# A gated hybrid decoder layer on one core: chunk states ordered ahead of VectorE's next work, output products one head later, silu and small copies on ScalarE, later modulation in blocks of 512 columns

## The chip, the cores and the metric

The kernel runs on one core of a Trainium2 chip. The metric is the device time of an execution in microseconds, as the median of runs. The engines are TensorE (PE in the views; PEld is its weight load), VectorE (DVE), ScalarE (ACT), GpSimd (POOL) and SyncE (SP), whose queue issues most transfers. Each engine takes its instructions in order.

## The reference

One layer for a prompt of 512 tokens and 64 sample tokens (8 sequences of 8), width 1024, all in 32 bits:

```python
mod = jax.nn.silu(c) @ w_ada + b_ada                  # shift1 scale1 gate1 shift2 scale2 gate2
u = x * (1 + sc1) + sh1
z = u @ w_in                                          # pool | q | f | i | out_gate | gate_A | gate_B
q = silu(z_q); f = lb + (1 - lb) * sigmoid(z_f); k = 1 - f; v = z_i      # 8 heads of 128
# per head, in chunks of 64 tokens, b = cumsum(log f) in the chunk:
att = tril((q * exp(b)) @ (k * exp(-b)).T);  o_intra = att @ v
S_c = exp(b_last) * S_(c-1) + (k * exp(b_last - b)).T @ v                # chunk states
o = o_intra + (q * exp(b)) @ S_(c-1)
y = o * rsqrt(mean(o * o) + eps) * hgrn_norm_w * silu(z_og)
merged = sigmoid(z_ga) * (y_pool @ w_a) + sigmoid(z_gb) * (y @ w_b)
x = layer_norm(ALPHA * x + g1 * (merged @ w_out))
h = x * (1 + sc2) + sh2
x = layer_norm(ALPHA * x + g2 * ((silu(h @ w_gate) * (h @ w_up)) @ w_down))
```

## The kernel before

Every large product is made in parts: a 32-bit matrix is split into a rounded high part (ScalarE's cast, tiles whi, hq) and a low rest (VectorE or GpSimd, tiles wlo, lq), and three products of the parts are added. On top of it `fast` (L217 to L250) makes two 1024-wide products at once by seven products of half size, p1 to p7, instead of eight; each has 12 matmuls of 288 columns (line L217). Its sums run on VectorE (L230), the first copy on ScalarE (L232); the seven results go through four banks of PSUM, tiles f. The callers hand in work to be written between the products: `mid` after the third, `end` after the fifth. `fast_w` loads the weights of the next pair by SyncE (L178) and prepares their sums on GpSimd (tiles st, L197 to L205) and their splits on all three (L172, L173); three buffers whi and wlo are shared by all, so a split waits until PE has left the one before.

In the loop over heads, pass h makes f and q of head h with one such pair and v and g (the output gate) with a second, while the recurrence of head h - 1 stands between: `hg1` transposes (L615 to L635), `hg2` makes the products within chunks, then the eight chunk states S one after another on VectorE (L663, each from the one before) and the sample states sn, `hg3` the outputs with their square root (L685 to L700), `hg4` turns the outputs back and multiplies by the gate. For head h, `ev_f` takes the sigmoid of f, runs the decay product as a scan (L559), three reciprocals (L562), kd (L564), GpSimd's kl (L566, L567) and its split klx; `ev_q`, `ev_qd`, `ev_i` and `ev_og` do the same for q, v (split vx) and g. `stack3` makes the splits klx and vx of the 64 sample columns.

Eight gate pairs follow. The first two carry the last head, the other six carry the rest of the modulation (`ada`, L339): shift2, scale2, gate1 and gate2, in 16 blocks of 256 columns. The feed-forward part (`ffn`) comes after the first layer norm, then the last product and norm.

The order on each engine is not the order of the code: a scheduler sets it when the program is built, by its own estimate of times; dependencies come from tiles. `tc.high_priority` lets instructions go ahead where they are ready; `tc.issue_after(ins)` keeps what a block writes for the engine of `ins` behind it. Line numbers are those of the kernel before; the changed kernel's lie up to some 30 lower or higher.

Of the kernel before, what the change touches and what calls it, by code (L numbers as in the profile page):

```python
# [73 lines left out]
def trunk(tc, consts, x_prompt, x_sample, state_pool, state_hgrn, c_prompt, c_sample,  # L74
# [254 lines left out]
    gada = {G1: t_(dr, [P, 4, 256], "gada1"), G2: t_(dr, [P, 4, 256], "gada2")}  # L329

    def ada(blk, pl_, psp, tag, raw=None):
# [12 lines left out]
        if G1 <= m < SH2 or m >= G2:  # L344
            base = G1 if m < SH2 else G2
            sp.dma_start(out=gada[base][:, (m - base) // 2], in_=ev)
            return
# [290 lines left out]
    def hg2(h):  # L638
# [36 lines left out]
        sp.dma_start(out=nhgrn_s[0, :, h].rearrange("b k v -> k b v"), in_=sn)

    def hg3(h):
# [616 lines left out]
```

## Time and profile before

| what | value |
|---|---|
| median of 3 runs | 1057.97 us (1055.69 to 1061.18) |
| profiled execution | 1058.36 us |
| its span, first to last instruction | 1056.6 us |
| mean granted clock of TensorE | 0.974 |
| PE busy | 987.5 us, 93% |
| VectorE busy | 828.6 us, 78% |
| ScalarE busy | 484.1 us, 46% |
| GpSimd busy | 368.6 us, 35% |

The span is what the trace shows; the profiled execution is 1.8 us longer than it. The stages, in us from the span's start: modulation, first products and pooling to 102; head 0's end and the first pass to 125; six passes to 341; the last head and gates 0 and 1 to 398; gates 2 to 7 with the later modulation to 490; the products with w_a, w_b and w_out and the first norm to 654; feed-forward products to 894; the last product and norm to the end. A busy share over the whole span hides that these stages have different limits, so it has to be read for each.

### The profile page before, as it was taken

To read this page: it belongs to the slowest core of one execution; us is meant where nothing else is said; L and a number is where in the kernel's file an instruction comes from. 1 tells how busy PE (TensorE), PEld (TensorE's weight loads), DVE (VectorE), ACT (ScalarE), POOL (GpSimd) and SP (SyncE) were. 2 spreads that over 40 slices of the span, in tenths; PEclk is the share of its full clock that TensorE was granted. 3 is DMA by queue.
4 is the path that set the end of the run, shared out by engine and by line. 5 is a ranking of instruction groups with operands and counts; after the bars stand their busy time and mean duration, and the time that the engine had idled before them with its cause. 6 is when DMAs were issued, how large, how long until landed. Compare 5 with 4: busy or idle time off the path is not lost.

```text
span 1056.6 us, 17662 instructions
## 1 busy us (share of the span) xinstructions
PE 987.5 (93%) x6803; PEld 897.7 (85%) x6803; DVE 828.6 (78%) x1433; ACT 484.1 (46%) x867; POOL 368.6 (35%) x269
## 2 busy tenths in 40 slices
PE   5999888989899899999988998999999999999993
PEld 3689888989899897788987677999999999788882
DVE  3563899879989966446899598999999999957428
ACT  3454564665466563334334344544434435633322
POOL 0013666657757554555364011112212210000004
PEclk7999999989999999999999999999999999999997
DMA  8940223323233229882324800232332333432202
GB/s 272 294 141 28 80 86 101 99 65 102 81 103 97 69 83 289 255 274 91 110 66 144 239 21 20 62 99 83 99 100 81 100 101 104 135 120 81 80 20 90
DMA packets 167143, 120.58 MB, mean 114 GB/s; under 512 B 4253, under 2 KB 154809, under 8 KB 167051
## 3 DMA queue, kind: packets, MB, share of 16 engines
q1 hardware_dynamic: 164719, 113.98, 35.9%
q10 hardware_dynamic: 2340, 5.47, 1.7%
q8 instruction: 53, 0.87, 0.3%
q14 instruction: 31, 0.25, 0.1%
HBM read 111.15 MB, written 8.40 MB: 113 GB/s over the span
## 4 chain that ended last, share of the span: by engine, by line
PE 65%; DVE 19%; DMA 6%; issue 4%; ACT 3%; POOL 2%; SPq 0%; DVEq 0%; POOLq 0%; ACTq 0%
PE b L217 24%; PE f L217 13%; DVE wlo L173 4%; PE b L1139 4%; PE b L1138 4%; PE b L1137 4%; DMA ada<-in_w_ada 3%; PE zp L421 3%; PE z L154 3%; DMA raw<-in_w_in 1%; PE s L339 1%; PE b L1143 1%; DVE S L663 1%; PE b L1142 1%; DVE g L230 1%
## 5 line engine op out<-in xcount | busy, mean ns | idle before, releaser
L172 ACT CAST whi<-st 128x512 fp32r<-128x512 f32 x184 | 109.0, 617 | 102.1 <-POOL st L203 25.2
L173 DVE TENSOR_TENSOR wlo<-st,whi 128x512 fp32r<-128x512 f32 x140 | 126.8, 927 | 8.8 <-ACT whi L172 4.2
L217 PE MATMUL f<-uh,whi 128*128 128x288 f32 x352 | 107.3, 305 | 0.0
L217 PE MATMUL f<-ul,whi 128*128 128x288 f32 x352 | 106.2, 302 | 0.0
L217 PE MATMUL f<-uh,wlo 128*128 128x288 f32 x352 | 106.0, 301 | 0.0
L197 POOL TENSOR_TENSOR st<-raw 128x512 f32<-128x512 f32 x36 | 50.3, 1398 | 155.4 <-DVE wlo L173 58.6
L112 DVE TENSOR_TENSOR wlo<-raw,whi 128x1024 fp32r<-128x1024 f32 (+1 forms) x49 | 57.9, 1181 | 35.9 <-ACT whi L111 35.3
L172 ACT CAST whi<-raw 128x1024 fp32r<-128x1024 f32 x46 | 48.3, 1049 | 78.0 <-PE f L217 37.4
L198 POOL TENSOR_TENSOR st<-st,raw 128x512 f32<-128x512 f32 x46 | 62.2, 1353 | 51.0 <-issue 49.5
L111 ACT CAST whi<-raw 128x1024 fp32r<-128x1024 f32 (+1 forms) x49 | 47.9, 978 | 65.6 <-PE b L1139 20.0
L1139 PE MATMUL b<-whi,hl 128*128 128x512 f32 (+1 forms) x198 | 72.6, 367 | 0.0
L1138 PE MATMUL b<-whi,hl 128*128 128x512 f32 (+1 forms) x198 | 72.5, 366 | 0.0
L1137 PE MATMUL b<-wlo,hl 128*128 128x512 f32 (+1 forms) x198 | 72.3, 365 | 0.0
L217 PEld LDWEIGHTS f<-uh,whi 128*128 128x128 f32 x352 | 67.4, 191 | 3.5 <-issue 1.6
L217 PEld LDWEIGHTS f<-ul,whi 128*128 128x128 f32 x352 | 67.3, 191 | 2.7 <-issue 2.5
L217 PEld LDWEIGHTS f<-uh,wlo 128*128 128x128 f32 x352 | 67.1, 191 | 2.1 <-issue 1.6
L203 POOL TENSOR_TENSOR st<-raw,st 128x512 f32<-128x512 f32 x26 | 40.6, 1561 | 75.5 <-DVE wlo L173 74.2
L173 DVE TENSOR_TENSOR wlo<-raw,whi 128x1024 fp32r<-128x1024 f32 x46 | 62.7, 1363 | 2.4 <-ACT whi L172 2.3
L173 POOL TENSOR_TENSOR wlo<-st,whi 128x512 fp32r<-128x512 f32 x44 | 59.0, 1358 | 11.2 <-ACT whi L172 5.3
L1206 POOL TENSOR_TENSOR x<-x,lg 128x640 f32<-128x640 f32 (+2 forms) x4 | 5.9, 1468 | 160.0 <-ACT x L1197 160.0
L217 PE MATMUL b<-bh,whi 128*128 128x288 f32 x184 | 55.4, 301 | 2.1 <-ACT bh L172 2.1
L217 PE MATMUL b<-bh,wlo 128*128 128x288 f32 x184 | 54.8, 299 | 0.0
(464 smaller groups left out, 3304.4 us busy)
## 6 DMA issues: line engine op xcount, KB each, us to landing
raw<-in_w_in SPq DMA_DIRECT2D x52, 512.0 KB
ada<-in_w_ada SPq DMA_DIRECT2D x48, 512.0 KB
raw<-in_w_gate SPq DMA_DIRECT2D x22, 512.0 KB
raw<-in_w_down SPq DMA_DIRECT2D x22, 512.0 KB
raw<-in_w_up SPq DMA_DIRECT2D x12, 512.0 KB
rawu<-in_w_up SPq DMA_DIRECT2D x10, 512.0 KB
s<-in_state_hgrn SPq DMA_DIRECT2D x8, 512.0 KB
out<-sn SPq DMA_DIRECT2D x8, 512.0 KB
```

The lines of the kernel that those rows point to most:

```text
L111: act.copy(out=hi[:, :n], in_=raw[:, :n])
L112: eng.tensor_tensor(out=lo[:, :n], in0=raw[:, :n], in1=hi[:, :n].bitcast(F32), op=ALU.subtract)
L154: mm = pe.matmul(out=ps[:, GA0 + c0:GA0 + c1], lhsT=a[:, kt * P:(kt + 1) * P], rhs=x[:, kt, c0:c1], start=first and i == 0, stop=last and ...
L172: act.copy(out=hi, in_=src)
L173: return eng.tensor_tensor(out=lo, in0=src, in1=hi.bitcast(F32), op=ALU.subtract)
L197: pool.tensor_tensor(out=s1, in0=a21, in1=a22, op=ALU.add)
L198: pool.tensor_tensor(out=s2, in0=s1, in1=a11, op=ALU.subtract)
L203: eng.tensor_tensor(out=s4, in0=a12, in1=s2, op=ALU.subtract)
L217: pe.matmul(out=ps, lhsT=x[:, k * P:(k + 1) * P], rhs=y[:, k], start=first and k + i == 0, stop=last and k == 3 and i == 2)
L1137: pe.matmul(out=o, lhsT=xh, rhs=lo, start=first, stop=False)
L1138: pe.matmul(out=o, lhsT=xl, rhs=hi, start=False, stop=False)
L1139: return pe.matmul(out=o, lhsT=xh, rhs=hi, start=False, stop=last)
```

## The change

Four things are done. On ScalarE, silu takes the place of a sigmoid that VectorE multiplied by its argument, for q, the output gate and the feed-forward gate, and the plain copies of `stack3` (klx, vx) move from VectorE to ScalarE. In a head, the chunk states get priority, and VectorE's sample sums and its whole second pair of products (with `ev_q`) are ordered behind the last state; `hg3` moves from after the third product of that pair to after the fifth, `hg4` from the end of the pass to the next pass (in gate 0 for head 6); the square root and reciprocal are taken once for prompt and samples. The later modulation runs in eight blocks of 512 columns, two in each of gates 2 to 4, one in gates 5 and 6 and none in gate 7, with two buffers of 1 MB in place of three of 0.5 MB; the tiles of gate 7 are allotted after they are closed.

```diff
     def ada_load(pl_, blk):
-            raw = t_(pl_, [P, 4, 256], "ada", bufs=8 if pl_ is s0 else 3)
+            raw = t_(pl_, [P, 4, 256], "ada", bufs=8)
...
-    gada = {G1: t_(dr, [P, 4, 256], "gada1"), G2: t_(dr, [P, 4, 256], "gada2")}
+    gada = {G1: t_(dr, [P, D], "gada1"), G2: t_(dr, [P, D], "gada2")}
...
-    q0_ = act.activation(out=q0, in_=z[:, ZR], func=AF.Sigmoid)
-    dve.tensor_tensor(out=q0, in0=z[:, ZR], in1=q0, op=ALU.mult)
+    q0_ = act.activation(out=q0, in_=z[:, ZR], func=AF.Silu)
...
     def stack3(x, tag, his, lo):
         for i in his:
-            dve.tensor_copy(out=o[:, :, 32 * i:32 * i + 32], in_=xs_)
+            act.copy(out=o[:, :, 32 * i:32 * i + 32], in_=xs_)
...
     def ev_q(h, q):
-            x = t_(ep, [P, T], "tmp", bufs=4)
-            act.activation(out=x, in_=q, func=AF.Sigmoid)
-            dve.tensor_tensor(out=q, in0=q, in1=x, op=ALU.mult)
+            act.activation(out=q, in_=q, func=AF.Silu)
...
     def ev_og(h, g):
-        s = t_(ep, [P, T], "tmp", bufs=4)
-        act.activation(out=s, in_=g, func=AF.Sigmoid)
-        dve.tensor_tensor(out=g, in0=g, in1=s, op=ALU.mult)
+        act.activation(out=g, in_=g, func=AF.Silu)
...
     def hg2(h):
-        act.copy(out=S[:, 0], in_=ps[0][:, 0:P])
-        for c in range(1, NCH):
-            o = (c // 2) * P
-            dve.scalar_tensor_tensor(out=S[:, c], in0=S[:, c - 1], scalar=s["p"][:, c * CH + CH - 1:c * CH + CH],
-                                     in1=ps[c % 2][:, o:o + P], op0=ALU.mult, op1=ALU.add)
+        with tc.high_priority():
+            act.copy(out=S[:, 0], in_=ps[0][:, 0:P])
+            for c in range(1, NCH):
+                o = (c // 2) * P
+                end = dve.scalar_tensor_tensor(out=S[:, c], in0=S[:, c - 1], scalar=s["p"][:, c * CH + CH - 1:c * CH + CH],
+                                               in1=ps[c % 2][:, o:o + P], op0=ALU.mult, op1=ALU.add)
...
-            dve.tensor_tensor(out=sn[:, 4 * r:4 * r + 4], in0=ps.rearrange("p (b v) -> p b v", b=4),
-                              in1=sn[:, 4 * r:4 * r + 4], op=ALU.add)
+            with tc.issue_after(end.ins):
+                dve.tensor_tensor(out=sn[:, 4 * r:4 * r + 4], in0=ps.rearrange("p (b v) -> p b v", b=4),
+                                  in1=sn[:, 4 * r:4 * r + 4], op=ALU.add)
+        return end
...
     def hg3(h):
-            act.activation(out=ms[:n, a:b], in_=ms[:n, a:b], func=AF.Sqrt, scale=1.0 / P, bias=epsr[:n])
-            dve.reciprocal(out=ms[:n, a:b], in_=ms[:n, a:b])
+        act.activation(out=ms, in_=ms, func=AF.Sqrt, scale=1.0 / P, bias=epsr)
+        dve.reciprocal(out=ms, in_=ms)
+        for x, n, o, a, b in tiles:
             dve.tensor_tensor(out=o, in0=x[:n, :(b - a) * P].rearrange("p (i v) -> p i v", v=P), in1=bcast(ms[:n, a:b], P),
                               op=ALU.mult)
...
+    def ada_late(m, pl_):
+        ps = st_()
+        for st in range(2):
+            raw = t_(pl_, [P, 4, 512], "ada", bufs=2)
+            sp.dma_start(out=raw, in_=w_ada[0][st * 512:(st + 1) * 512, m * P:m * P + 512].rearrange("(k p) n -> p k n", p=P))
+            for g in range(4):
+                pe.matmul(out=ps[32 * g:32 * g + 32], lhsT=cpad[:, st * 4 + g, :], rhs=raw[:, g, :],
+                          start=st == 0, stop=st == 1, tile_position=(0, 32 * g))
+        ev = t_(pl_, [P, 512], "adaev")
+        dve.tensor_copy(out=ev, in_=ps)
...
     for h in range(1, NH):
         f, q = (t_(ep, [P, T], "tmp", bufs=4) for i in range(2))
-        fast_u(f, q, lambda: hg1(h - 1), lambda: ev_f(h, f))
-        hg2(h - 1)
-        ev_q(h, q)
-        v, g = vg()
-        fast_u(v, g, lambda: hg3(h - 1), lambda: (ev_qd(h), ev_i(h, v)))
-        hg4(h - 1)
+        def mid():
+            if h > 1:
+                hg4(h - 2)
+            hg1(h - 1)
+
+        fast_u(f, q, mid, lambda: ev_f(h, f))
+
+        with tc.issue_after(hg2(h - 1).ins):
+            ev_q(h, q)
+            v, g = vg()
+            fast_u(v, g, None, lambda: (hg3(h - 1), ev_qd(h), ev_i(h, v)))
         ev_og(h, g)
...
-    gate(0, lambda: hg1(NH - 1))
+    gate(0, lambda: (hg4(NH - 2), hg1(NH - 1)))
...
     for m in range(2, KT):
-        for i in range(3 if m < 6 else 2):
-            ada(ada_todo.pop(0), adap, psB, "s")
+        for i in range(2 if m < 5 else 1 if m < KT - 1 else 0):
+            ada_late(ada_todo.pop(0), adap)
...
     def swiglu(m, j, g, u):
-        act.activation(out=x, in_=g, func=AF.Sigmoid)
-        dve.tensor_tensor(out=x, in0=g, in1=x, op=ALU.mult)
+        act.activation(out=x, in_=g, func=AF.Silu)
...
     def ffn(m, q):
-        act.activation(out=x, in_=AC[m], func=AF.Sigmoid)
-        dve.tensor_tensor(out=x, in0=AC[m], in1=x, op=ALU.mult)
+        act.activation(out=x, in_=AC[m], func=AF.Silu)
```

By the built programs' order, ScalarE has 32 table loads before and 38 now; the six passes from the scan of head 1 to that of head 7 hold 20 before and 24 now.

VectorE, in the pass of head 4, some dozen instructions behind its scan (p; the order prints a scan as SCALAR_TENSOR_TENSOR), before: g and v are the tiles that collect the second pair's products, tmp and f others of them, wlo the low part of weights, on the normalised outputs.

```order
L230 TENSOR_TENSOR g_2511<-f_2622,g_2511 128x288
L663 SCALAR_TENSOR_TENSOR S_2488<-S_2488,p_2009,s_2479 128x128
L173 TENSOR_TENSOR wlo_2519<-st_2522,whi_2518 128x512
L575 CAST klx_2436<-kl_2433 128x2x32 x2
L173 TENSOR_TENSOR wlo_2519<-st_2523,whi_2518 128x512
L663 SCALAR_TENSOR_TENSOR S_2488<-S_2488,p_2009,s_2478 128x128
L592 TENSOR_TENSOR qs_853<-tmp_2283,p_2425 128x8x8
L576 TENSOR_TENSOR klx_2436<-kl_2433,klx_2436 128x2x32
L699 RECIPROCAL ms_2609<-ms_2609 64x1
L663 SCALAR_TENSOR_TENSOR S_2488<-S_2488,p_2009,s_2479 128x128
L700 TENSOR_TENSOR on_2610<-s_2587,ms_2609 64x128
L663 SCALAR_TENSOR_TENSOR S_2488<-S_2488,p_2009,s_2478 128x128
```

The same place now, from the first state on.

```order
L658 SCALAR_TENSOR_TENSOR S_2468<-S_2468,p_1996,s_2459 128x128
L562 TENSOR_TENSOR kd_2411<-tmp_2398,tmp_2407 128x576
L658 SCALAR_TENSOR_TENSOR S_2468<-S_2468,p_1996,s_2458 128x128
L658 SCALAR_TENSOR_TENSOR S_2468<-S_2468,p_1996,s_2459 128x128
L658 SCALAR_TENSOR_TENSOR S_2468<-S_2468,p_1996,s_2458 128x128
L658 SCALAR_TENSOR_TENSOR S_2468<-S_2468,p_1996,s_2459 128x128
L658 SCALAR_TENSOR_TENSOR S_2468<-S_2468,p_1996,s_2458 128x128
L574 TENSOR_TENSOR klx_2416<-kl_2413,klx_2416 128x2x32
L658 SCALAR_TENSOR_TENSOR S_2468<-S_2468,p_1996,s_2459 128x128
L669 TENSOR_TENSOR sn_2478<-s_2480,sn_2478 128x512
L669 TENSOR_TENSOR sn_2478<-s_2483,sn_2478 128x512
L173 TENSOR_TENSOR wlo_2495<-raw_2490,whi_2494 128x1024
```

The states (S, L663 before, L658 now) stood one by one between splits, casts and adds; now six follow each other, the seventh behind klx's subtract, and the sample sums, the split of the weights and the adds of the second pair come behind.

ScalarE, in the pass of head 5, from the splits of weights (whi, hq) to the first copy of the next pass's products (COPY tmp, f), before: o and ms belong to the squares and their sums.

```order
L172 CAST whi_2936<-st_2948 128x512
L172 CAST whi_2936<-st_2950 128x512
L697 ACTIVATE o_555_3024,ms_3025<-s_3002 128x128
L172 CAST hq_2956<-raw_2930 128x512
L697 ACTIVATE o_555_3024,ms_3025<-s_3002 128x128
L599 ACT_TABLE_LOAD
L599 ACTIVATE tmp_3111<-g_2927 128x576
L697 ACTIVATE o_555_3024,ms_3025<-s_3002 128x128
L232 COPY tmp_3114<-f_3148 128x288
L697 ACTIVATE o_555_3024,ms_3025<-s_3002 128x128
L698 ACT_TABLE_LOAD
L698 ACTIVATE ms_3025<-ms_3025,eps_79 128x4
```

Now:

```order
L573 CAST vx_3037<-v_2897 128x2x32
L695 ACTIVATE o_545_3023,ms_143_858<-s_3001 128x128
L573 CAST vx_3037<-v_2897 128x2x32
L695 ACTIVATE o_545_3023,ms_143_858<-s_3001 128x128 x3
L172 CAST whi_2907<-st_2919 128x512
L696 ACT_TABLE_LOAD
L696 ACTIVATE ms_143_858<-ms_143_858,eps_79 128x5
L172 CAST whi_2907<-st_2921 128x512
L172 CAST hq_2927<-raw_2901 128x512
L594 ACT_TABLE_LOAD
L594 ACTIVATE g_2898<-g_2898 128x576
L232 COPY tmp_3071<-f_3105 128x288
```

The four squares, the root and the gate's activation stand in the same stretch; the two casts of vx (L575 before, on VectorE) have come between the squares, and the root's second load has gone behind one for both parts.

SyncE, at gate 2, before: ada are the modulation's weights, raw the gates' weights, in the order of issue.

```order
L257 DMA ada_4376<-in_w_ada 128x4x256
L257 DMA ada_4392<-in_w_ada 128x4x256
L257 DMA ada_4394<-in_w_ada 128x4x256
L178 DMA raw_4601<-in_w_in 128x8x128
L257 DMA ada_4545<-in_w_ada 128x4x256
L257 DMA ada_4547<-in_w_ada 128x4x256
L178 DMA raw_4786<-in_w_in 128x8x128
L257 DMA ada_4563<-in_w_ada 128x4x256
L257 DMA ada_4565<-in_w_ada 128x4x256
L257 DMA ada_4581<-in_w_ada 128x4x256
L257 DMA ada_4583<-in_w_ada 128x4x256
L257 DMA ada_4734<-in_w_ada 128x4x256
```

Now:

```order
L178 DMA raw_4347<-in_w_in 128x8x128
L721 DMA ada_4304<-in_w_ada 128x4x512
L721 DMA ada_4310<-in_w_ada 128x4x512
L178 DMA raw_4522<-in_w_in 128x8x128
L721 DMA ada_4325<-in_w_ada 128x4x512
L178 DMA raw_4524<-in_w_in 128x8x128
L721 DMA ada_4331<-in_w_ada 128x4x512
L178 DMA raw_4689<-in_w_in 128x8x128
L721 DMA ada_4481<-in_w_ada 128x4x512
L721 DMA ada_4487<-in_w_ada 128x4x512
L178 DMA raw_4691<-in_w_in 128x8x128
L721 DMA ada_4502<-in_w_ada 128x4x512
```

Where two to six loads of half a megabyte stood between two gate weights, one or two of a megabyte do now.

## Rows read from the trace of the kernel before

**Rows 1.** the page: busy us, share of the span, instructions by engine
```profile
PE 987.5 (93%) x6803; PEld 897.7 (85%) x6803; DVE 828.6 (78%) x1433; ACT 484.1 (46%) x867; POOL 368.6 (35%) x269
```

**Rows 2.** windows: us, busy by engine, granted clock, DMA share, GB/s
```profile
125.29:340.68 215.39, 200.86 (x1528) 193.31 (x1528) 193.82 (x348) 125.67 (x254) 144.16 (x103) 0.98 0.31 91
...
198.07:235.21 37.14, 33.38 (x234) 32.13 (x232) 31.27 (x58) 20.96 (x42) 21.97 (x16) 0.91 0.27 80
...
340.68:398.00 57.32, 53.66 (x418) 51.96 (x417) 44.80 (x81) 35.08 (x73) 32.43 (x26) 1.00 0.31 89
...
398.00:489.72 91.72, 89.79 (x757) 72.35 (x756) 43.55 (x85) 31.57 (x51) 45.67 (x35) 1.00 0.82 248
...
654.00:894.00 240.00, 240.00 (x1800) 239.72 (x1800) 237.58 (x365) 104.03 (x176) 49.37 (x38) 1.00 0.31 90
```

**Rows 3.** waits of PE in 125.29:340.68, then in 340.68:398.00
```profile
PE s L691 <- DVE S L663: 10.9, 12, 1.7
...
PE s L691 <- DVE S L663: 2.8, 3, 1.6
```

**Rows 4.** waits of VectorE in 125.29:340.68
```profile
DVE g L600 <- ACT tmp L599: 5.4, 5, 2.2
...
DVE ms L699 <- ACT ms L698: 4.5, 4, 1.7
```

**Rows 5.** groups by line, VectorE, 125.29:340.68
```profile
L600 DVE TENSOR_TENSOR g<-g,tmp 128x576 f32<-128x576 f32 x6 | 7.6, 1260 | 5.4 <-ACT tmp L599 5.4
...
L575 DVE CAST vx<-v 128x64 fp32r<-128x64 f32 x12 | 5.5, 498 | 0.0
...
L583 DVE TENSOR_TENSOR tmp<-tmp,tmp 128x576 f32<-128x576 f32 x6 | 4.6, 763 | 0.0
...
L575 DVE CAST klx<-kl 128x64 fp32r<-128x64 f32 x12 | 3.9, 368 | 0.0
```

**Rows 6.** timeline of VectorE, the last head
```profile
340.68 1.39 DVE L559 TENSOR_TENSOR_SCAN p<-tmp,d 128x576 f32<-128x576 f32 x1
...
342.11 3.78 DVE L562 RECIPROCAL tmp<-p 128x192 f32<-128x192 f32 x3
...
348.36 0.75 DVE L564 TENSOR_TENSOR kd<-tmp,tmp 128x576 f32<-128x576 f32 x1
...
357.82 0.44 DVE L230 TENSOR_TENSOR v<-f,g 128x288 f32<-128x288 f32 x1
...
359.82 0.34 DVE L663 SCALAR_TENSOR_TENSOR S<-S,p,s 128x128 f32<-128x128 f32 x1
```

**Rows 7.** timeline of GpSimd, the same head
```profile
349.18 1.06 POOL L566 TENSOR_TENSOR kl<-kd,p 128x512 f32<-128x512 f32 x1 [4.61 <-DVE kd L564]
...
350.20 1.29 POOL L567 TENSOR_TENSOR kl<-kd,p 128x64 f32<-128x64 f32 x1
```

**Rows 8.** timeline of ScalarE, the last two heads
```profile
326.03 1.28 ACT L599 ACT_TABLE_LOAD   x1
...
327.32 0.69 ACT L599 ACTIVATE tmp<-g 128x576 f32<-128x576 f32 x1
...
365.32 0.38 ACT L232 COPY sga<-f 128x288 f32<-128x288 f32 x1
```

**Rows 9.** timeline of PE, later modulation
```profile
406.05 0.64 PE L339 MATMUL s<-ada,cpad 128*32 128x256 f32 x8
...
406.62 0.40 PE L217 MATMUL f<-t4h,lq 128*128 128x288 f32 x1
...
446.05 1.50 PE L339 MATMUL s<-ada,cpad 128*32 128x256 f32 x24
```

**Rows 10.** windows, the loads of the later modulation
```profile
395.00:465.00 70.00, 69.11 (x586) 53.81 (x585) 34.90 (x65) 24.86 (x41) 38.64 (x31) 1.00 0.92 278
```

**Rows 11.** groups by line, VectorE, whole span
```profile
L1074 DVE TENSOR_TENSOR sg<-ac,sg 128x576 f32<-128x576 f32 x12 | 8.9, 743 | 0.0
...
L1041 DVE TENSOR_TENSOR sg<-b,sg 128x288 f32<-128x288 f32 x4 | 1.8, 445 | 0.0
```

More of the change, by code (lines that the diff above doesn't have):

```diff
@@ L334, in ada @@
             raw = ada_load(pl_, blk)
-        ps = t_(psp, [P, 512], tag, bufs=2 if tag == "t" else 4)
+        ps = t_(psp, [P, 512], tag, bufs=2)
         for st in range(2):
@@ L343, in ada @@
         dve.tensor_copy(out=ev, in_=ps[:, :256])
[L344 to L347, printed above, removed]
         for j in range(2):
@@ L537, in trunk @@
     qss = qs.rearrange("p (b x) -> p b x", x=QW)[:, :, 0:LS]
+    MS = [t_(hp, [P, 5], f"ms{i}") for i in range(2)]
+    for x in MS:
+        pool.memset(x, 1.0)
     vmk = cst[:96, C_BM:C_BM + 4]
@@ L692, in hg3 @@
         o2 = t_(hp, [P, P], "o2", bufs=2)
-        ms = t_(hp, [P, 5], "ms", bufs=2)
+        ms = MS[h % 2]
         on = t_(hp, [P, 5, P], "on")
-        for x, n, o, a, b in ((px, TS, on[:TS, 4:5], 4, 5), (ps, P, on[:, 0:4], 0, 4)):
+        tiles = (px, TS, on[:TS, 4:5], 4, 5), (ps, P, on[:, 0:4], 0, 4)
+        for x, n, o, a, b in tiles:
             for i in range(a, b):
                 act.activation(out=o2[:n], in_=x[:n, (i - a) * P:(i - a + 1) * P], func=AF.Square, accum_out=ms[:n, i:i + 1])
-            act.activation(out=ms[:n, a:b], in_=ms[:n, a:b], func=AF.Sqrt, scale=1.0 / P, bias=epsr[:n])
-            dve.reciprocal(out=ms[:n, a:b], in_=ms[:n, a:b])
+        act.activation(out=ms, in_=ms, func=AF.Sqrt, scale=1.0 / P, bias=epsr)
+        dve.reciprocal(out=ms, in_=ms)
+        for x, n, o, a, b in tiles:
             dve.tensor_tensor(out=o, in0=x[:n, :(b - a) * P].rearrange("p (i v) -> p i v", v=P), in1=bcast(ms[:n, a:b], P),
@@ L715, in hg4 @@
                                  op0=ALU.mult, op1=ALU.mult)
-    ada_todo = [SC2 // 2 + b for b in range(4)] + [SH2 // 2 + b for b in range(4)] + \
-               [G1 // 2 + b for b in range(4)] + [G2 // 2 + b for b in range(4)]
+    def ada_late(m, pl_):
[8 more added lines that the diff above has]
+        dve.tensor_copy(out=ev, in_=ps)
+        if G1 <= m < SH2 or m >= G2:
+            base = G1 if m < SH2 else G2
+            sp.dma_start(out=gada[base][:, (m - base) * P:(m - base) * P + 512], in_=ev)
+            return
+        px = st_()
+        for j in range(4):
+            pe.matmul(out=px[:, 16 * j:16 * j + 9], lhsT=ev[:, j * P:(j + 1) * P],
+                      rhs=cst[:, C_SEL:C_SEL + 9], start=True, stop=True)
+        dve.tensor_tensor(out=mod[:, m:m + 4], in0=px[:, :64].rearrange("p (j c) -> p j c", j=4)[:, :, 0:9],
+                          in1=bcast(prow[:, R_BA + m:R_BA + m + 4], 9), op=ALU.add)
+    ada_todo = [SC2, SC2 + 4, SH2, SH2 + 4, G1, G1 + 4, G2, G2 + 4]
     pairs = iter([(win(a + h), win(b + h)) for h in range(1, NH) for a, b in ((M_F, M_Q), (M_I, M_OG))] +
@@ L777, in trunk @@
     pl.close(_hp)
-    _sgb = sg_open(KT - 2)
+    _sgb = sg_open(KT - 3)
     yah, _yah = pl.open("yahl", "right")
@@ L783, in trunk @@
     for m in range(2, KT):
-        for i in range(3 if m < 6 else 2):
-            ada(ada_todo.pop(0), adap, psB, "s")
+        for i in range(2 if m < 5 else 1 if m < KT - 1 else 0):
+            ada_late(ada_todo.pop(0), adap)
+        if m == KT - 1:
+            pl.close(_adap)
+            _sgc = sg_open(1)
         gate(m)
@@ L791, in trunk @@
             prefetch(2)
-    pl.close(_adap)
     pl.close(_wu)
@@ L844, in trunk @@
             split_act(MM[:, m + i], a)
-    for c in (_wy, _yt, _yah, _sgb, _sga, _psF, _psB):
+    for c in (_wy, _yt, _sgc, _yah, _sgb, _sga, _psF, _psB):
         pl.close(c)
@@ L872, in gate_bc @@
         ga = t_(pool_, [P, D], "ga")
-        act.dma_start(out=ga, in_=gada[mb].rearrange("p a b -> p (a b)"))
+        act.dma_start(out=ga, in_=gada[mb])
         act.dma_start(out=ga[R_BIAS:R_BIAS + 1], in_=b_ada[0:1, mb * P:mb * P + D])
```

## The prediction

> **What bounds the kernel now.** The page comes first [rows 1]: the reader sees the matrix engine (PE) busy 93% of the span and VectorE 78%, so the two must be read stage by stage. The windows do that [rows 2]. From 654 to 894, the feed-forward products, PE is busy 240.00 of 240.00 us: nothing that another engine saves there can show. From 398.00 to 489.72, the late gates with the later modulation, PE is busy 89.79 of 91.72 while the DMA engines are at 0.82. The loop over heads is different. The stretch 125.29 to 340.68 runs from the scan of one head to the scan six heads later, so a head takes 215.39 / 6 = 35.9 us; PE is busy 200.86 / 6 = 33.5 of it and VectorE 193.82 / 6 = 32.3. Neither is full: they wait for each other. One head (198.07 to 235.21) also shows a granted clock of 0.91. PE's waits tell the main cause [rows 3]: 10.9 us in twelve waits are for the chunk states S (L663), 1.8 per head, and 2.8 more follow in 340.68 to 398.00. VectorE in turn waited 5.4 us for ScalarE's sigmoid of g (L599) and 4.5 us for the square root (L698) [rows 4].
>
> **The change part by part.**
>
> *VectorE work in a head.* Removed per head: the multiply L600 (1.26 us), L583 (0.76), two casts of vx (2 x 0.498) and two of klx (2 x 0.368), together 3.75 us; with one 64-row reciprocal it is some 3.9 [rows 5]. These means hold time lost to GpSimd's traffic, so less may come free. The chunk states now stand together: in the last head of before the scan began at 340.68 and the last state at 359.82, 19.1 us later, with splits and adds between [rows 6]. Now they follow the reciprocals, so S is there some ten microseconds sooner and the 1.8 us that PE waited for it per head should go. SyncE's store of S also leaves sooner, and the weight loads queued behind it. This 1.8 is not a second gain beside the 3.9: it is the same lateness, seen from PE.
>
> *What is late next.* First, klx. Its subtract now stands on VectorE before the last state, and its casts are ScalarE's. Counted from the scan: scan 1.4, reciprocals 3.8, one state 0.35 and kd 0.75 give 6.3 us [rows 6]; GpSimd's two kl products take 1.06 + 1.29, to 8.7 [rows 7]; the casts end near 9.2. VectorE has by then done five more states of 0.33 and stands at 8.0: it waits 1.2 us, and behind this wait stand the last state, the sample sums, the weight splits and the adds that free PE's banks. An old trace cannot show a ScalarE cast of 128x64: it costs more than nothing and less than the 0.38 of a 128x288 copy [rows 8]; I take 0.25, nearer the copy because the columns are few but an instruction has a fixed part. Second, ScalarE's chain. From v's fifth add (ends 358.2) to the first copy of the next products (365.32) it took 7.1 us [rows 6, 8]: squares, root, table loads, sigmoid, in order. The vx casts now stand inside it, 0.5 us. By the program's order these six heads hold 24 table loads instead of 20; at 1.28 each [rows 8] that is 0.86 more per head, of which I put half, 0.4, on the chain, since a load may run while its operand is awaited; uncovered, all of it counts. Silu itself I price as the sigmoid it replaces, 0.69 [rows 8].
>
> *Sum for a head.* 3.9 - 1.2 - 0.5 - 0.4 = 1.8; I take 1.3, since some of the 3.9 is time lost to GpSimd that another instruction will then lose. The bounds: nothing regained, 0; or all that PE does not fill, 35.9 - 33.5 = 2.4. Six heads give 7.8 us (0 to 14.5).
>
> *Ends of the loop.* In 340.68 to 398.00 PE's 2.8 us for S [rows 3] mostly go: 1.5 (0 to 3). Before 125.29 the first head drops the same casts and multiplies but ScalarE gains a load of 1.28 before the silu of head 0: 0.5 (-1.3 to 2). Together 2.0. Output products of a head (hg4) now stand one head later; they stand between PE's products as before and g has two buffers, so I cost this at nothing. The normalised outputs that they read now depend on one square root for both parts; were those late, PE would wait in every head, up to the 0.75 (4.5 / 6) that VectorE waits for the root [rows 4].
>
> *Later modulation.* Before, 32 groups of eight PE rows; one group costs 0.57 (406.05 to 406.62) and three in a row 1.43, 0.48 each, so 0.1 of a group and some 0.2 of restart around it are overhead of switching [rows 9]. Sixteen groups of double width then cost about 0.95 + 0.3 instead of 2 x 0.77: 0.29 x 16 = 4.6 us less. The bounds of a wide group, which no row shows, are 0.48 and 1.14; I take 0.95, twice the bare group. Against that, the same 16.8 MB must now arrive within five gates instead of six: between the first and the last wide group the order gives PE 349 product matmuls, at 240.00 / 1800 = 0.133 each [rows 2], fifteen groups and the small ones, about 67 us, in which fifteen loads (15.7 MB) and some 4.5 MB of gate weights must land: 300 GB/s. Before, the pace in the busy part was 278 GB/s at a DMA share of 0.92 [rows 10]. At 278 it takes 72.7, so 5.7 us of waiting, where PE was idle 91.72 - 89.79 = 1.9 before [rows 2]. Net 4.6 - 5.7 + 1.9 = 0.8; I take 1 (-8 to 6; the low end is the whole stage's 248 GB/s, 81 us). The load of a gate's weights is behind two of the big ones on SyncE's queue, so such a wait would reach the gate products too.
>
> *Silu in the feed-forward part.* Twenty multiplies of 0.74 leave VectorE [rows 11], 15 us; PE's unbroken 240 us [rows 2] hide them, and 15 us is what could show if that cover were gone. At its start four multiplies of 0.445 [rows 11] stand ahead of operands that PE waits for: 1 us (0 to 1.8).
>
> *Sum.* 7.8 + 2.0 + 1 + 1 = 11.8 us. The profiled execution took 1058.4 us, of which the span is 1056.6; it becomes 1046.6. The median of the runs is 0.4 lower, so **1046 us**. The likeliest case's own range is 1038 to 1052.
>
> A rule speaks against the change. The table load of 1.28 us ends at 327.31, and the activation begins at 327.32 [rows 8]: nothing follows the load here. The Trainium skill, page "ScalarE: Activation LUTs", section "What ACT_TABLE_LOAD costs", gives 1283 ns for the load, as here, but 1380 ns of drain besides, 2.66 us per switch, and asks to batch by table set. By it the four loads of a head would be 10.6 us of ScalarE and not 5.1, and two more drains on ScalarE's chain in every head would bring the time to some 1065; by the trace's 1.28 it stays at 1046, and the trace does not show the drain.
>
> **The rivals.**
> *All coupling goes* (0.20). PE waits for nothing and the clock stays whole: 2.4 x 6 + 3 + 3 + 1.8 = 22.2 us, 1036 (to 1031). For it: PE's waits were nearly all one cause. Against: klx and ScalarE's chain.
> *The gain is handed back* (0.20). The loop is one of latency: what VectorE saves it waits. Only 3 us remain outside the heads: 1055 (1052.7 to 1059).
> *ScalarE's queue becomes the loop* (0.12), slower. Place: from v's fifth add to the first copy of the next products. It was 7.1 us; I expect 8.0. At 9.3 the 1.3 us of a head are gone; beyond that each us costs 1 us in every head. If the casts, which wait in order for v, hold the squares and both loads back so that it takes 11, a head takes 37.6: 6 x 1.7 more, less 2 elsewhere, 8 us, 1066. For it: ScalarE waits in order, and the casts stand between squares whose data are ready. Against: it is busy 125.67 of 215.39 us [rows 2].
> *Table loads at double price* (0.03). If each load held the next activation as long again, two more times 1.28 lie on the same chain, 8.0 to 10.6, and a head takes 37.2: 6 x 1.3 more, less 2 elsewhere, 1064. Against: the 0.01 us behind the load [rows 8]. The Trainium skill's section named above would have it so.
>
> **How the numbers follow.** The forecast has 0.45. About 0.5%, 5.3 us, is what a measurement of this kernel can tell from no change. Faster: 0.45 + 0.20 + 0.02 of the third case = 0.67; within: 0.20, of the third case and the edge of the first; slower: 0.13. The range leaves out the two slow cases (0.15) and the far end of the best (0.05): 1031 to 1058.
>
> **What would show it.** Right: PE's wait for S near zero; scan to scan 34 to 35 us; VectorE's busy time in six heads down by some 20 us; a new wait of klx's subtract for ScalarE, 1 to 2 us per head; loads in the late gates above 278 GB/s. Wrong: scan to scan still 35.9, with VectorE idle where it was busy; PE waiting for adds that free its banks; PE's waits for modulation loads above 8 us in total; or the clock below 0.95 in more heads than one.

## The result and the profile after

The changed kernel takes 1027.9 us in the median of 4 runs (1026.67 to 1030.82); the kernel before took 1059.15 beside it. The ratio is 0.972, 95% interval 0.968 to 0.976. Forecast were 1046 us and the range 1031 to 1058: the direction was right, the gain 2.6 times as large, and the time lies below the range. The profiled span fell from 1056.6 to 1025.6 us:

| stage, bounded by marks of both timelines | before | after | less | predicted less |
|---|---|---|---|---|
| start to the scan of head 0 | 102.1 | 99.0 | 3.1 | 0 |
| to the scan of head 1 | 23.2 | 20.9 | 2.3 | 0.5 |
| six heads, to the scan of head 7 | 215.4 | 198.8 | 16.6 | 7.8 |
| to gate 0's first sigmoid | 30.9 | 28.3 | 2.6 | 1.5 |
| to the same of gate 7 | 115.4 | 107.8 | 7.6 | 1 |
| to the end | 569.6 | 570.7 | -1.1 | 1 |

First the page's busy times, in answer to [rows 1]:

```profile
PE 973.9 (95%) x6675; PEld 888.9 (87%) x6675; DVE 785.0 (77%) x1341; ACT 495.6 (48%) x897; POOL 366.5 (36%) x271
```

Then windows of the stages, with the columns of [rows 2]: six heads, one of them, the last head with gates 0 and 1, the late gates, the feed-forward products.

```profile
119.93:318.77 198.84, 193.74 (x1533) 187.31 (x1532) 175.52 (x308) 134.55 (x283) 140.09 (x104) 1.00 0.35 100
220.05:252.97 32.92, 32.26 (x256) 31.28 (x255) 29.37 (x51) 21.84 (x47) 23.32 (x18) 1.00 0.35 99
318.77:368.42 49.65, 48.97 (x389) 47.91 (x387) 34.50 (x69) 29.72 (x67) 30.70 (x23) 1.00 0.28 81
368.42:457.40 88.98, 88.14 (x656) 72.41 (x656) 43.48 (x77) 34.95 (x56) 49.84 (x38) 1.00 0.83 268
...
621.78:863.10 241.32, 241.32 (x1799) 241.32 (x1800) 226.50 (x344) 108.51 (x178) 50.55 (x38) 0.99 0.31 91
```

In the six heads PE is now busy 97% at a granted clock of 1.00 (93% at 0.98 before), and VectorE has 18.3 us less work. In the feed-forward part PE is as unbroken as before, so the VectorE time saved there is invisible. PE's waits in the six heads, then VectorE's (us, times, longest):

```profile
PE s L680 <- DVE S L658: 3.6, 5, 0.9
PE s L680 <- DVE klx L574: 0.6, 1, 0.6
...
DVE tmp L230 <- ACT tmp L232: 7.2, 6, 2.0
DVE tmp L552 <- ACT tmp L551: 6.5, 6, 1.6
DVE tmp L230 <- PE f L217: 6.2, 6, 1.1
```

PE's wait for S fell from 10.9 us [rows 3] to 3.6. VectorE's waits for the sigmoid of g and for the root [rows 4] are gone; it never waits for ScalarE's casts of klx. The next rows are one head from its scan on VectorE, then GpSimd, then ScalarE (start, duration).

```profile
252.97 1.36 DVE L557 TENSOR_TENSOR_SCAN p<-tmp,d 128x576 f32<-128x576 f32 x1
...
258.45 0.75 DVE L562 TENSOR_TENSOR kd<-tmp,tmp 128x576 f32<-128x576 f32 x1
259.12 1.88 DVE L658 SCALAR_TENSOR_TENSOR S<-S,p,s 128x128 f32<-128x128 f32 x5
260.91 0.23 DVE L574 TENSOR_TENSOR klx<-kl,klx 128x64 fp32r<-128x64 f32 x1
261.05 0.34 DVE L658 SCALAR_TENSOR_TENSOR S<-S,p,s 128x128 f32<-128x128 f32 x1
...
266.44 0.45 DVE L230 TENSOR_TENSOR v<-f,g 128x288 f32<-128x288 f32 x1
...
259.28 1.06 POOL L564 TENSOR_TENSOR kl<-kd,p 128x512 f32<-128x512 f32 x1 [2.48 <-DVE kd L562]
260.30 0.31 POOL L565 TENSOR_TENSOR kl<-kd,p 128x64 f32<-128x64 f32 x1
...
260.63 0.39 ACT L573 CAST klx<-kl 128x64 fp32r<-128x64 f32 x2 [2.50 <-POOL kl L565]
...
266.92 0.25 ACT L573 CAST vx<-v 128x64 fp32r<-128x64 f32 x1 [3.29 <-DVE v L230]
...
269.16 1.28 ACT L696 ACT_TABLE_LOAD   x1
270.46 0.30 ACT L696 ACTIVATE ms<-ms,eps 128x5 f32<-128x5 f32 x1
...
271.81 1.28 ACT L594 ACT_TABLE_LOAD   x1
273.41 0.69 ACT L594 ACTIVATE g<-g 128x576 f32<-128x576 f32 x1 [0.32 <-DVE g L230]
274.00 0.38 ACT L232 COPY tmp<-f 128x288 f32<-128x288 f32 x1
```

The last state begins 8.1 us after the scan, against 19.1 in the head of [rows 6]. The klx casts are done as VectorE ends its five states. From the end of v's fifth add (266.89) to the first copy of the next products (274.00) ScalarE's chain took 7.1 us, as long as before although the casts stand in it.

### The profile page after: what moved, and what is told of

It is laid out like the page before. It is cut to its first block, busy times and chain, and to the rows that moved or that the text cites. A ratio compares the mean times of both kernels' runs of the same rounds, so it can differ in the third digit from the quotient of the medians.

```text
span 1025.6 us, 17312 instructions
## 1 busy us (share of the span) xinstructions
PE 973.9 (95%) x6675; PEld 888.9 (87%) x6675; DVE 785.0 (77%) x1341; ACT 495.6 (48%) x897; POOL 366.5 (36%) x271
## 4 chain that ended last, share of the span: by engine, by line
PE 65%; DVE 18%; DMA 5%; issue 5%; ACT 4%; POOL 2%; SPq 0%; POOLq 0%; DVEq 0%; ACTq 0%
PE b L217 24%; PE f L217 12%; PE b L1164 4%; PE b L1163 4%; PE b L1162 4%; PE z L154 3%; PE zp L417 3%; DMA ada<-in_w_ada 2%; DVE tmp L560 2%; ACT whi L172 2%; DVE wlo L173 2%; PE s L723 1%; DVE S L658 1%; PE b L1168 1%; PE b L1167 1%
## 5 line engine op out<-in xcount | busy, mean ns | idle before, releaser
L173 DVE TENSOR_TENSOR wlo<-st,whi 128x512 fp32r<-128x512 f32 x140 | 113.8, 838 | 9.4 <-ACT whi L172 4.2
L197 POOL TENSOR_TENSOR st<-raw 128x512 f32<-128x512 f32 x36 | 53.5, 1487 | 142.2 <-DVE wlo L173 61.4
L173 DVE TENSOR_TENSOR wlo<-raw,whi 128x1024 fp32r<-128x1024 f32 x46 | 58.6, 1274 | 19.0 <-ACT whi L172 18.9
L217 PE MATMUL b<-bl,whi 128*128 128x288 f32 x184 | 54.6, 297 | 0.0
```

The lines of the kernel that those rows point to most:

```text
L173: return eng.tensor_tensor(out=lo, in0=src, in1=hi.bitcast(F32), op=ALU.subtract)
L197: pool.tensor_tensor(out=s1, in0=a21, in1=a22, op=ALU.add)
L217: pe.matmul(out=ps, lhsT=x[:, k * P:(k + 1) * P], rhs=y[:, k], start=first and k + i == 0, stop=last and k == 3 and i == 2)
```

## The experiments

My theory after the result: a head is set by VectorE's queue, so the 18.3 us of work taken from it are the 16.6 us. The rival: it is set by the order in which the states stand. For the gates: the wide block saves PE's switching, or the distribution does it, or the loop ahead does. Six heads means the stretch from the scan of head 1 to that of head 7; ratios are to the kernel before on the same chip. The heads of one order differ between executions: in the order of before six heads took 215.4, 214.4 and 212.9 us (before, modulation alone, ffn_silu), in that of the changed kernel 198.8 to 199.3 in four runs.

| version | us | ratio, 95% interval | six heads | PE waits for S | VectorE waits for root | table loads in six heads |
|---|---|---|---|---|---|---|
| before | 1059.15 | | 215.4 | 10.9 | 4.5 | 20 |
| changed | 1027.9 | 0.968 to 0.976 | 198.8 | 3.6 | 0 | 25 |
| modulation alone | 1047.74 | 0.984 to 0.996 | 214.4 | 9.7 | 3.9 | 20 |
| changed, old modulation | 1036.38 | 0.976 to 0.985 | 199.3 | 3.5 | 0 | 25 |
| silu and copies alone | 1070.44 | 1.007 to 1.017 | 228.0 | 12.6 | 23.8 | 31 |
| ordering alone | 1060.94 | 1.001 to 1.007 | 217.6 | 3.6 | 0 | 12 |
| changed, copies on VectorE | 1038.34 | 0.977 to 0.986 | 204.2 | 7.1 | 0 | 24 |
| changed, sigmoid and multiply | 1039.85 | 0.979 to 0.986 | 207.3 | 4.3 | 0.2 | 12 |
| changed, hg3 and hg4 at old places | 1035.49 | 0.975 to 0.983 | 204.6 | 3.8 | 0 | 25 |
| changed, states not ordered | 1059.01 | 0.999 to 1.005 | 223.4 | 12.6 | 18.1 | 19 |
| the same, with sample sums last | 1028.56 | 0.969 to 0.977 | 195.3 | 0 | 11.7 | 18 |
| silu, copies, sample sums last | 1040.47 | 0.976 to 0.985 | 201.8 | 0 | 15.3 | 19 |
| silu, copies, silu of g behind root | 1057.29 | 0.994 to 1.000 | 217.0 | 13.8 | 2.4 | 25 |

**The halves.** Modulation alone, and all but the modulation:

```diff
# mod_only: of the diff ahead, ada_late, its loop and its tiles
+    for i in range(2 if m < 5 else 1 if m < KT - 1 else 0):
+        ada_late(ada_todo.pop(0), adap)
# no_mod: everything else
```

> The kernel before with the later modulation of the change alone (wide blocks, its distribution and buffers). Theory M, the late gates gain by the blocks themselves: gate 0's sigmoid to gate 7's sigmoid 117 us becomes 110, the whole 6 to 9 us faster. Rival, the late gates gain because the loop in front of them leaves less behind: at most 2 us faster, and the wide groups wait for their loads by about the 5.7 us of the prediction. Head to head stays 35.9 us by both. First z product by 66.5 us if the change set the earlier start, by 63.5 if the start differs from execution to execution.

> The changed kernel with the later modulation of before (256 columns, three buffers, six gates). Theory M: 6 to 9 us slower than the changed kernel, some 1035 us; head to head 33.1 us. Rival, the gain of the late gates comes from the loop: within 2 us of the changed kernel, 1028 to 1030.

Theory M held: 8.5 us between no_mod and the changed kernel, and some 11 (4 to 17 by the interval) for the modulation alone, with the heads unchanged. Gate 0 to gate 7 took 109.5 us in the one and 116.0 in the other. mod_only, whose code ahead of the heads is that of before, also has its first scan at 99.0: the earlier start is a difference between executions.

```diff
# silu_copies: before, with
+    act.copy(out=o[:, :, 32 * i:32 * i + 32], in_=xs_)
+    act.activation(out=q, in_=q, func=AF.Silu)        # and g, and the feed-forward gate
# order_only: before, with hg2, hg3, hg4 and the loop of the change
```

> The kernel before with silu and the small copies on ScalarE, in the order of before. Theory W, a head is set by VectorE's work: most of the 16.5 us of the six heads comes with it, head to head 33.5 to 34, the whole 10 to 15 us faster, PE's wait for S shrinks by itself. Rival O, a head is set by the late chunk states: head to head stays at 35 or above, PE still waits 8 us or more for S, the whole 2 to 5 us faster.

> The kernel before with the ordering alone: chunk states first, VectorE's next pair behind them, output products later, one square root for both parts; the multiplies and copies stay on VectorE. Theory W: PE's wait for S falls under 4 us, but head to head only falls to 35 to 35.5, since VectorE then holds up the adds; 3 to 6 us faster. Rival O: head to head 33.5 to 34, 10 to 15 us faster.

Both theories failed. Each part alone gains nothing, the first loses 12 us, and together (no_mod) they gain 22. Silu and copies alone took 18.8 us of work from VectorE in the six heads (175.00 busy) and lengthened them by 12.6: work removed is not time gained. The waits of PE and VectorE in silu and copies alone, 123.1:351.1:

```profile
PE s L686 <- DVE S L658: 12.6, 11, 2.1
PE s L667 <- DVE atp L643: 6.8, 6, 1.4
...
DVE ms L694 <- ACT ms L693: 23.8, 6, 4.3
```

and the timeline of its ScalarE at the end of one head:

```profile
258.28 1.28 ACT L595 ACT_TABLE_LOAD   x1
259.57 0.69 ACT L595 ACTIVATE g<-g 128x576 f32<-128x576 f32 x1
260.28 1.28 ACT L693 ACT_TABLE_LOAD   x1
261.57 0.30 ACT L693 ACTIVATE ms<-ms,eps 128x4 f32<-128x4 f32 x1
```

Silu of g stands ahead of the root, each with a table load, and VectorE's reciprocal, at the head of its queue, waits 4 us a head. Six heads hold 31 table loads here, 20 before. Ordering alone has the opposite trouble: the states are early, but v's adds are late. VectorE is busy 197.1 of 217.6 us, and v's fifth add begins 18.8 us after the scan (249.73 in the head from 230.90), against 13.5 in the changed kernel; the multiply of q, splits, qs and qz stand ahead of it. PE waits for v's adds in 122.3:339.9:

```profile
PE f L217 <- DVE v L230: 12.6, 6, 2.8
PE s L689 <- DVE S L667: 3.6, 5, 1.0
```

**Taking one part out of the changed kernel.**

```diff
# no_copies
+    dve.tensor_copy(out=o[:, :, 32 * i:32 * i + 32], in_=xs_)
# no_silu
+    act.activation(out=x, in_=q, func=AF.Sigmoid)
+    dve.tensor_tensor(out=q, in0=q, in1=x, op=ALU.mult)      # and for g
# hg34_old
+    fast_u(v, g, lambda: hg3(h - 1), lambda: (ev_qd(h), ev_i(h, v)))
+    hg4(h - 1)
# no_order: neither high_priority nor issue_after
+    hg2(h - 1); ev_q(h, q); v, g = vg()
+    fast_u(v, g, None, lambda: (hg3(h - 1), ev_qd(h), ev_i(h, v)))
```

> The changed kernel with the small copies of klx and vx back on VectorE; silu, ordering and modulation stay. The ordering alone left PE waiting 14.8 us in six heads for the second pair's adds, behind VectorE's work. Theory P, every microsecond of that work counts: the copies are 1.7 of the 3.9 us of a head, so a head goes from 33.1 to 34.3 to 34.6 us and the whole to 1034 to 1037. Rival T, a threshold: with silu gone VectorE is early enough, a head stays within 0.4 us of 33.1 and the whole within 3 us of 1028.

> The changed kernel with the sigmoid and VectorE's multiplies of before in the heads (the feed-forward silu stays); copies on ScalarE, ordering and modulation stay. Theory P: the multiplies are 2.0 us of a head, head to head 34.5 to 34.8 us, the whole 1036 to 1039. Rival T: a head within 0.4 us of 33.1, the whole within 3 us of 1028; it could even gain, since the heads then hold about half of the 25 table loads of the changed kernel.

> The changed kernel with the outputs and their transposes (hg3, hg4) at their places of before: hg3 after the third product of the second pair, hg4 at the end of the pass. Theory A, ScalarE's order decides: with silu and copies alone VectorE waited 23.8 us for the square root behind silu and its table load; with hg3 at the old place that comes back, a head takes 35 us or more and the whole 1040 or more. Rival S, the states ahead of VectorE's next pair decide: a head within 0.5 us of 33.1, the whole within 3 us of 1028.

> The changed kernel without the priority of the chunk states and without VectorE's second pair ordered behind them; hg3 and hg4 at the later places, one square root, silu, copies and modulation stay. Theory A: the root stays early on ScalarE, a head takes 33.1 to 33.8 us, the whole 1028 to 1032. Rival S: the states are late again, PE waits some 10 us for S in six heads, a head takes 35 us or more, the whole 1039 or more.

Theory P held within 1.4 us of its whole times: with the states in order, VectorE's work counts (5.4 and 8.5 us of the six heads). The prices of [rows 5] make 10.4 and 12.1, but VectorE's busy time rose by only 4.8 us (180.3 against 175.5) and 7.6 (183.1): what the work took here shows in full. In no_silu VectorE also waits 12.5 us for the sigmoid of g, so that not all of its 8.5 need be work. no_silu holds 12 table loads in the six heads, the changed kernel 25, and is slower. The old places of hg3 and hg4 cost 5.7 us of the heads, between the two theories: PE waits 5.8 us for the normalised outputs, and VectorE for no root. The order is the largest: without it six heads take 24.5 us more, beyond rival S.

**What of the order it is.**

```diff
# no_prio: states without tc.high_priority()
# prio_only: second pair outside the block
-        with tc.issue_after(hg2(h - 1).ins):
+        hg2(h - 1)
# hg3_late: hg3 behind the pair
+            fast_u(v, g, None, lambda: ev_i(h, v)); hg3(h - 1); ev_qd(h)
# mod256_front: blocks of 256 columns in the distribution of the change
+        for i in range(4 if m < 5 else 2 if m < KT - 1 else 0):
```

> The changed kernel without the priority of the chunk states; VectorE's second pair (and the sample sums) stay ordered behind the last state. Theory, the order of the second pair is what carries the 31 us that the kernel without both lost: a head stays within 0.4 us of 33.1, the whole within 3 us of 1028. Rival, the priority carries it: states stand between first-pair adds, splits and the klx subtract again, PE waits 8 us or more for S in six heads, the whole 1036 or more.

> The changed kernel with the priority of the chunk states (and sample sums behind the last), but the second pair free to go ahead of them. Theory, the order of the second pair carries it: VectorE's states stand apart again with adds and splits between, the root is late, a head takes 36 us or more, the whole 1045 or more. Rival, the priority carries it: a head within 0.5 us of 33.1, the whole within 4 us of 1028.

> The changed kernel with the outputs of a head (hg3) moved on from after the fifth product of the second pair to behind that pair, and qz and qs of the next head behind them. PE still waited 3.6 us for S in six heads of the changed kernel. Theory, that wait is all that is left to take: it goes, a head takes 32.5 us, the whole 1024 to 1026. Rival, the later squares and root hold up the transposes of hg4 and the later qz holds up the products within chunks: a head takes 33.5 us or more, the whole 1030 or more.

> The changed kernel with the later modulation in blocks of 256 columns and three buffers as before, but in the distribution of the change (four blocks in each of gates 2 to 4, two in gates 5 and 6, none in gate 7). Theory R, what the wide block saves is PE's switching, 4 to 5 us, and the longer rows that let the loads keep up: PE waits 4 us or more for modulation loads, the gates take 114 us or more, the whole 1034 to 1040. Rival, the distribution gives the gain: the gates take 110 us or less, the whole 1027 to 1031.

no_prio took 1029.64 us (0.969 to 0.976), but it proves less than it was meant to: it is the changed kernel instruction for instruction, in the same order on every engine, so the priority does nothing and the run is a repeat. prio_only refuted its theory: the second pair may go ahead. Since the priority does nothing, its text is that of no_order with one line more, the two sample sums behind the last state, and it is 30 us faster. That line moves more than the two sums, because the scheduler sets every order anew: of VectorE's 306 instructions in the six heads only 223 stand in the order of no_order, of ScalarE's 271 only 203. The timeline of VectorE in a head of no_order, whose scan begins at 228.81:

```profile
235.99 1.28 DVE L667 TENSOR_TENSOR sn<-s,sn 128x512 f32<-128x512 f32 x2
...
241.07 2.64 DVE L173 TENSOR_TENSOR wlo<-st,whi 128x512 fp32r<-128x512 f32 x2
243.63 1.28 DVE L574 TENSOR_TENSOR klx<-kl,klx 128x64 fp32r<-128x64 f32 x1
...
246.57 0.72 DVE L657 SCALAR_TENSOR_TENSOR S<-S,p,s 128x128 f32<-128x128 f32 x2
```

and in a head of prio_only, whose scan begins at 251.01:

```profile
261.94 0.22 DVE L574 TENSOR_TENSOR klx<-kl,klx 128x64 fp32r<-128x64 f32 x1
...
262.70 1.28 DVE L173 TENSOR_TENSOR wlo<-st,whi 128x512 fp32r<-128x512 f32 x2
263.90 0.34 DVE L658 SCALAR_TENSOR_TENSOR S<-S,p,s 128x128 f32<-128x128 f32 x1
264.16 1.28 DVE L669 TENSOR_TENSOR sn<-s,sn 128x512 f32<-128x512 f32 x2
```

With the sums early the last state begins some 18 us after the scan, with the sums last 12.9. The place of the sums themselves is only 1.28 of this: five states instead of two stand ahead of the 128x1024 split, the two splits shown halved and the klx subtract fell from 1.28 to 0.22. In the six heads VectorE is busy 167.1 us with what took 176.5. hg3_late met its rival, at its edge: S was no longer waited for, yet the heads took 201.1 us and the whole 1030.18 (0.970 to 0.976), PE waiting 5.7 us for atp instead. mod256_front took 1036.81 us (0.976 to 0.985), its gates 116.8: the distribution gives nothing. But PE waited only 1.9 us for its loads, so the second half of theory R, that long rows are needed to keep up, fell.

**The switch, from the other side,** starting from before, and the feed-forward part by itself:

```diff
# silu_copies_sn: silu_copies and; sn_only: before and
+            with tc.issue_after(end.ins):      # end: the last state
                 dve.tensor_tensor(out=sn[:, 4 * r:4 * r + 4], ...)
# silu_copies_root: silu_copies and
+        with tc.issue_after(H[h - 1]["root"].ins):
             ev_og(h, g)
# ffn_silu: before and
+        act.activation(out=x, in_=AC[m], func=AF.Silu)      # and in swiglu
```

> The kernel before with silu and small copies on ScalarE, and of all the ordering only the two sample sums behind the last chunk state. Theory N, the sums ahead of the states are the switch: the states stand closer together, PE's wait for S falls from 12.6 to under 5 us, a head takes 33 to 34.2 us instead of 38, the whole 1036 to 1042. Rival, the square root is the switch (hg3 still after the third product, VectorE waits for the root behind ScalarE's silu): VectorE still waits 15 us or more for it, a head takes 36 us or more, the whole 1052 or more.

> The kernel before with only the two sample sums behind the last chunk state; the multiplies and copies stay on VectorE. Theory N with the load: VectorE has 193 us of work in 215, and the sums then hold back the adds behind them, so nothing comes of it: head to head 35.5 to 36.5, the whole within 5 us of before. Rival, the sums alone are the whole effect: a head takes 34 us or less, the whole 1045 or less.

> The kernel before with silu and small copies on ScalarE, and of all the ordering only the silu of the output gate kept behind the square root of the head before on ScalarE. Theory root: VectorE's wait for the root falls from 23.8 us to under 10 and a head takes 36 us or less, the whole 1058 or less. Rival, theory N: the states stay where they are, PE still waits 10 us or more for S, a head takes 37 us or more, the whole 1064 or more.

> The kernel before with silu in the feed-forward part alone. The prediction's cover, PE busy 240 of 240 us, holds: nothing in the feed-forward part, at most 1 us at its start, the whole within 2 us of before. Rival, VectorE's 15 us there came back in part: the whole 4 us or more faster.

Theory N held as far as the edit goes: with silu and copies, the one line that puts the two sums last turns 1070 into 1040 us and gives back 26 us of the heads, although VectorE still waits 15.3 us for the root. The windows of six heads without it and with it:

```profile
123.10:351.10 228.00, 206.20 (x1529) 197.28 (x1528) 175.00 (x313) 144.14 (x293) 140.91 (x103) 0.95 0.29 86
...
121.40:323.20 201.80, 193.68 (x1533) 187.46 (x1531) 161.22 (x314) 129.46 (x281) 144.76 (x103) 1.00 0.34 98
```

What the line does is not separated further. More than a quarter of VectorE's instructions stand in another order; the last state begins 12.2 us after the scan instead of 17.7; VectorE takes 13.8 us less for the same work; PE is busy 12.5 us less with the same products, at a granted clock of 1.00 instead of 0.95; and ScalarE has 19 table loads instead of 31. With the multiplies and copies on VectorE the line gives little (1056.58, 0.994 to 0.999; six heads 217.7, PE waiting 11.9 us for v and g). The root is a second cause: behind it, silu of g gives back 11 us of the heads, with S as late as ever (13.8). Six table loads go there too, so within these three versions the loads are a rival that no run takes alone (31, 25 and 19 for 1070, 1057 and 1040 us). Against it, no_order and prio_only hold 19 and 18 and differ by 30 us, and the changed kernel holds 25. The feed-forward silu gave 1058.06 us (0.995 to 1.000): at most some 5 us by the interval, and its products took 255.7 us from first to last matmul against 255.9, so nothing in that part. Its heads are those of before, instruction for instruction, and yet:

```profile
122.50:335.40 212.90, 197.14 (x1527) 189.00 (x1526) 193.58 (x349) 125.10 (x254) 143.29 (x103) 1.00 0.32 92
```

That is 2.5 us under [rows 2] at a clock of 1.00 instead of 0.98: up to 2.5 of the 16.6 us lie between executions.

## Why the prediction was right in sign and wrong in size

**VectorE work in a head: the step that failed.** The prediction's sum, "3.9 - 1.2 - 0.5 - 0.4 = 1.8; I take 1.3", measured 2.76 a head (up to 0.4 of it lies between executions). VectorE gave up 3.05 (18.3 / 6): of the 3.9, 0.85 came back in its other instructions, where 0.5 was allowed. The three subtractions came to nothing:
- "it waits 1.2 us" for klx: VectorE ended its five states 8.0 us after the scan, as worked out, but the casts were done then too, not at 9.2. The second kl product took 0.31 us; the 1.29 of [rows 7] was its price beside one of VectorE's splits (349.28 to 351.32).
- "0.5 us" of casts and "0.4" of loads on ScalarE's chain: the chain kept its 7.1 us, with 25 loads in the six heads where 24 were expected and 20 stood before. ScalarE waited 18.7 us for PE before its squares in the heads of before, and 7.3 after, so I take the casts to lie in that idle time; no run shows it alone.

The split beside that kl product, and ScalarE's waits before its squares, of before; then the wait of after:

```profile
349.28 2.04 DVE L173 TENSOR_TENSOR wlo<-raw,whi 128x1024 fp32r<-128x1024 f32 x1
...
ACT o L697 <- PE s L685: 12.2, 6, 2.5
...
ACT o L697 <- PE s L691: 6.5, 3, 3.4
...
ACT o L695 <- PE s L682: 7.3, 6, 1.3
```

**The upper bound** "all that PE does not fill, 35.9 - 33.5 = 2.4" was no bound: PE's busy time was itself stretched. PE is busy 32.3 a head now, at a clock of 1.00, and 32.9 at that clock in the very heads of before (ffn_silu).

**The reasoning beneath the sum** was also wrong, and its size came near VectorE's 3.05 for another reason. The prediction called the wait for S "not a second gain" and priced VectorE's work as the gain, at a fixed order. The runs show that neither removal nor order is worth anything alone (+12.6 us of the heads, and +2.2, no more than executions of one order differ by), that both together give the gain, and that the larger part of the order hangs on one line, the two sums behind the last state, with all that it moves. That S would come "some ten microseconds sooner" was right (11).

**Ends of the loop:** 4.9 instead of 2.0, the same term mis-sized; the first pass took 20.9 us with silu and copies alone too, so its 2.3 needs no ordering. **Start:** 3.1 us that no step held, and that mod_only has too, with the start of before: executions differ there; the window of the first 40 us before, at a granted clock of 0.79,

```profile
0.00:40.00 40.00, 28.41 (x159) 18.29 (x160) 14.35 (x46) 13.45 (x19) 0.52 (x5) 0.79 0.94 297
```

and after, at 1.00:

```profile
0.00:40.00 40.00, 29.91 (x172) 20.03 (x173) 17.31 (x50) 15.53 (x21) 0.52 (x5) 1.00 0.96 305
```

**Later modulation:** 7.6 us instead of 1. PE's saving (4.6) was about right; "At 278 it takes 72.7, so 5.7 us of waiting" failed. The timeline of PE after, a wide group and the product behind it:

```profile
376.52 1.06 PE L723 MATMUL s<-ada,cpad 128*32 128x512 f32 x8
377.51 0.40 PE L217 MATMUL f<-ul,whi 128*128 128x288 f32 x1
```

windows from the first wide group to the last, and of the densest loads:

```profile
376.59:445.05 68.46, 67.62 (x505) 52.89 (x509) 31.00 (x58) 24.43 (x39) 40.70 (x31) 1.00 0.88 286
...
400.00:428.00 28.00, 28.00 (x212) 22.27 (x210) 12.31 (x23) 10.06 (x16) 14.93 (x12) 1.00 0.93 303
```

and PE's wait for modulation loads in gate 0 to gate 7:

```profile
PE s L723 <- DMA ada<-in_w_ada: 0.8, 2, 0.6
```

A bare wide group costs 0.99, close to the 0.95 taken. The time between products beyond their pace of 0.133, summed over all breaks, fell from 26.8 us in 30 breaks to 21.6 in 17. The 278 of [rows 10] was a mean at a DMA share of 0.92, not a limit: 303 were moved at 0.93. The remaining 2.4 us of the gates I have not traced. **FFN start:** the 1 us did not show.

**The rivals.** "ScalarE's queue becomes the loop" (1066) is what half the change does: silu and copies alone took 1070. The casts are not the reason: they stay where silu of g behind the root gives back 11 of the 12.6 us. The place of the root and the six table loads that go with it are not told apart. The order of the other half takes it away. "Table loads at double price" did not happen in any version: where its operand is there, an activation follows its load after 0.01 to 0.02 us (259.57, 270.46). The Trainium skill, page "ScalarE: Activation LUTs", section "What ACT_TABLE_LOAD costs", has a drain besides; no run here shows it. "All coupling goes" (1036) was nearest, with its bound too high for the reason above.

## What to carry to other kernels

Where engines take turns in a loop, price a change by the order in which its instructions will stand, not by the busy time it removes: here the same removal lengthened six heads by 12.6 us or shortened them by 13.6, by one line that puts two additions last. Compare the whole order, too: such a line moved more than a quarter of VectorE's instructions, so the two additions are the handle and need not be the cause. A wait at the head of an in-order queue (a reciprocal for a root) is found in the queue of the engine that it waits for. Neither PE's busy time at a clock below 1 nor a mean DMA rate is a floor or a ceiling.

## What the hardware showed that was not expected

A VectorE instruction with both inputs in SBUF, the on-chip memory of the tiles, had no fixed price while GpSimd worked beside it. Between before and after, the 128x512 split went from 1069 to 699 ns in the mean and the 128x256 product qz from 802 to 1558, both within the six heads; the 128x64 klx subtract took 0.22 us in one order and 1.28 in another. It goes with whether GpSimd is in the middle of an instruction when VectorE's begins. The long klx subtract (243.63 to 244.91) began inside this one, which ends at 244.82:

```profile
243.25 1.57 POOL L203 TENSOR_TENSOR st<-raw,st 128x512 f32<-128x512 f32 x1 [0.69 <-DVE wlo L173]
```

In the six heads of before, the 14 splits of 128x512 that began with GpSimd between instructions took 0.67 to 0.69 us, the ten others 0.79 to 2.40 (not every such start costs: in prio_only four of nine kept 0.67 to 0.68). VectorE's instructions that read a product from PSUM, the memory that PE writes, kept their price in either case: the states 0.25 to 0.35 us, the adds of the pairs 0.43 to 0.46. The contention did not go, it moved, and the order decides on what it falls. Versions whose heads lost time to waits also showed granted clocks of 0.95 to 0.99 there (0.95 for silu and copies alone, 0.96 for no_order), the fast ones 1.00; but the heads of before ran at 0.98 or 1.00 in different executions, so the clock follows the waits in tendency only.
